# Sums of h made inside the up product and kept in DRAM, and retention's last head loading the first K tiles of its down product

## The chip, the cores and the metric

The kernel runs on 1 core of one Trainium2 chip. The metric is the device time of one execution in microseconds (us); the number compared is the median of the runs. Engines are named as in the profile: PE (TensorE, matrix products), PEld (its weight loads), DVE (VectorE), ACT (ScalarE), POOL (GpSimd), SP (SyncE, which issues nearly all the DMAs, in order).

## The reference, cut to what matters

```python
# two layers, rows = 1024 prompt frames and 32 sample frames, D = 1024, D_FF = 2816, float32
for i in range(2):
    h = rmsnorm(x, norm_mix[i])
    x = x + (retention_mixer if i == 0 else gla_mixer)(h, ...)
    x = x + conv_ffn(rmsnorm(x, norm_ffn[i]), ...)
y = rmsnorm(x, norm_final)

def retention_mixer(h, S0, pos, w_in, gn_g, w_out):      # 4 heads, dk = 256, dv = 512
    q, k, v, g = split(h @ w_in)                          # q, k rotated
    S, o = run_chunked(step, S0, (q, k, v))               # per head, chunk by chunk, with a state S
    o = (o - mean(o)) * rsqrt(var(o) + EPS) * gn_g        # per frame and head
    return (silu(g) * o) @ w_out, S                       # w_out: 2048 x 1024

def conv_ffn(h, conv_state, w_up, conv_w, conv_b, w_down):
    u = h @ w_up                                          # 1024 x 5632
    c = conv_b + sum(ext[:, j:j+T] * conv_w[j] for j in range(3))
    gate, val = split(c)
    return (silu(gate) * val) @ w_down, ext[:, T:]        # w_down: 2816 x 1024
```

The states and the last rows of each convolution are outputs too.

## The kernel before, in words

T = 1056 columns (1024 prompt, 32 sample) stand on the free axis, in four chunks `CQ` of TH = 264; features stand on the 128 partitions. Every float32 product is made of three matmuls on values split in two parts: hi times hi, hi times lo, lo times hi. A split is an ACT copy to the hi part (`CAST`) and a DVE subtraction for the lo part. So an operand is ready in two steps on two engines, and a matmul can start on the hi part when the lo part isn't there yet.

The stages in order of time, in the profiled execution:

1. Opening and the q, k, g products of retention, to 359 us.
2. Retention (`retention`), 359 to 715 us: 4 heads of 9 chunks, the last chunk of a head the 32 sample rows. `chunk` is a generator whose parts are run in turns with those of the next chunk. A head's weights `w_rv` are loaded when it starts (`Head`). After the chunks m = 1, 3, 5, 7 of each head `weight_sums_out` (L352) loads two pieces of `w_down`, makes four sums of them on DVE and stores them in the DRAM scratch `scr_w`. They use the same ring of `raw` tiles as the weight loads. The retention pool gives PSUM's eight banks in the order in which its tiles are first asked for: four to `sm`, one to `v` (psv), one to `out` (po), two to `pu`.
3. Retention's down product (`second(0)`, class `Down`, L1197), 715 to 884 us: 16 K tiles, for each chunk of 264 columns 8 output tiles, each in a PSUM bank of its own; per K tile 8 x 3 matmuls (L1260, L1261, L1262). `Down.early` (L1205) loads and splits the first two K tiles while the last chunk of retention runs. `Down.load` (L1224) loads the weights (`raw<-w_ro`) and h (`AR<-scr_or`, L1234), and splits both (L104 and L1236/L1237; `XB` is the room in which the hi and lo parts stand).
4. The up product of layer 0 (`ffn_up`, L1444), 884 to 1371 us: 22 pairs f of feature tiles, each with two halves s of the columns and 7 products for each half instead of 8 (a Strassen-Winograd scheme; `seven`, L327 to L332). A product is 12 matmuls of 264 columns. `conv` (L1470) convolves, gates, and stores h of this f in the DRAM scratch `scr_h` (L1487, L1488).
5. The down product's first 16 K tiles, in the same scheme (class `Pieces`), 1371 to 1585 us: part p = 0 takes h of f 0 to 7, part p = 1 of f 8 to 15. A unit (p, q, s) is one pair q of output tiles and one half s. Its right operands are seven blocks of h and of sums of h, split in hi and lo, in the rooms `X[s][1..7]` that lie in XA and XB. The loads of h (`staged`, L1341, 1056 KB each) and `operands` (L1343), a list of 7 splits and 4 subtractions on DVE (L1355, 128x1056 each) per s, are made at the transition: those of (p 0, s 0) in the last f of the up product, those of (p 0, s 1) in `run` before its first unit, through the same two staging rooms `SX` in the tile AR.
6. The last 6 K tiles (`Down`), 1585 to 1640 us. Then GLA and the same stages 3 to 6 for layer 1 to the end (its transition from up to down at 2637 us).

The order of the engines' instructions is set by a scheduler that knows the dependencies and the program's order; each engine then works through its list in order, and SP issues DMAs in order. The waits named below are therefore waits of a whole engine.

Of the kernel before, what the change touches and what calls it, by code (L numbers as in the profile page):

```python
# [52 lines left out]
def trunk_kernel(ctx: ExitStack, tc: tile.TileContext, io):  # L53
# [201 lines left out]
    scr_x = io["scr_x"]  # L255
    scr_w, scr_g, scr_qk = io["scr_w"], io["scr_g"], io["scr_qk"]
# [370 lines left out]
    def retention(d1):  # L627
# [13 lines left out]
        def first_loads():  # L641
# [6 lines left out]
            for c in range(2):  # L648
                c0, n = CM[c]
                for j in (1, 0):  # L650
# [3 lines left out]
                    o += 768  # L654

# [14 lines left out]
        rmask, rcol = early[:2]  # L670
        last_v = [None]
# [29 lines left out]
        def chunk(H, m):  # L701
# [68 lines left out]
            if norms:  # L770
                norms.pop()(rsm)
            po = pp.tile([P, RDV], F32, tag="out", name=f"po{i}")
# [5 lines left out]
            pu = pp.tile([P, 2, RDV], F32, tag="pu", name=f"pu{i}")  # L778
# [35 lines left out]
            if end:  # L814
                on = w_tile(f"on{i}").bitcast(F32)
                sg = w_tile(f"sg{i}").bitcast(F32)[:, :RDV]
            else:
                on = rp.tile([P, RDV], F32, tag="on", name=f"on{i}", bufs=2)
                sg = rp.tile([P, RDV], F32, tag="sg", name=f"sg{i}", bufs=3)
            sg = sg.rearrange("p (e t) -> p e t", e=4)  # L820
# [3 lines left out]
            def norm(sm):  # L824
# [3 lines left out]
                if end:  # L828
                    ot = on[:, RDV:].rearrange("p (e t) -> p e t", e=4)
                else:  # L830
                    ot = rp.tile([P, 4, P], F32, tag="ot", name=f"ot{i}", bufs=2)
# [4 lines left out]
            if m % 2 == 1:  # L836
                j = 4 * h + m // 2
# [4 lines left out]
        heads = {0: Head(0)}  # L842
        run = chunk(heads[0], 0)
        next(run)
        for n in range(len(units)):
# [8 lines left out]
            else:  # L854
                d1.early(0)
                d1.early(1)
            next(run)
            if n in (0, 2):
# [345 lines left out]
    class Down:  # L1204
        def __init__(self, nk, wsrc, hsrc, chunks, res, sm, keep, hold):  # L1205
# [4 lines left out]
        def early(self, kt):  # L1210

            c0, n = self.chunks[0]
            hr = raw_tile(f"he{uid()}")[:, :n]
            nc.sync.dma_start(hr, self.hsrc(kt)[:, c0:c0 + n])
            h = w_tile(f"hs{uid()}")
            S.copy(h[:, :n], hr)
            V.tensor_tensor(h[:, 512:512 + n], hr, h[:, :n].bitcast(F32), op=ALU.subtract)
            w = load_w(self.wsrc(kt))
            if kt in self.keep:
                self.kept[kt] = w  # L1220
            self.ops[0, kt] = w, (h, h[:, 512:])
# [18 lines left out]
        def run(self, room, evict, norm_a, norm_b, done, nxt=()):  # L1240
# [3 lines left out]
            for c, (c0, n) in enumerate(self.chunks):  # L1244
                xr = room("xr")[:, :KT * n].rearrange("p (k t) -> p k t", k=KT)
                nc.sync.dma_start(xr, self.res[:, :, c0:c0 + n])
# [585 lines left out]
```

## Time and profile before

| | |
|---|---|
| median of 3 runs | 2894.62 us (2890.69 to 2897.35) |
| the profiled execution, its own time | 2897.01 us |
| its span in the trace | 2895.2 us (1.8 us lie outside it) |
| mean granted TensorE clock | 0.988 |
| busy: PE, PEld | 2800.4 us (97%), 2695.0 us (93%) |
| busy: DVE, ACT, POOL | 2143.6 us (74%), 1333.6 us (46%), 294.0 us (10%) |
| DMA queue q1 | 399.48 MB, 41.8% of the 16 DMA engines' time |

A row of the timeline gives the start, the length, the engine, the line, the operation, `out<-in` by the program's names, the shapes, and in brackets the engine's idle time just before the instruction with what ended it. Matmuls overlap: of two that follow each other at full rate the starts lie 0.12 us apart for 264 columns, though each is recorded as 0.28 us long.

### The profile page before, as it was taken

The page shows a single profiled execution, that of the slowest core. Times are in us where ns is not written, and L with a number is a line of the kernel's source. Part 1 is how long each engine was busy: PE and PEld are TensorE (multiplying, and loading weights), DVE is VectorE, ACT ScalarE, POOL GpSimd, SP SyncE. Part 2 cuts the span into 40 slices and gives each one's busy share as a digit, 9 for nine tenths or more (in the row PEclk, how much of TensorE's full clock was granted, in tenths as well). Part 3 has the DMA queues.
Part 4 walks back from the last instruction along what each step waited for, and adds up shares of the span by engine and source line. Part 5 has one row for each costly group of instructions (what it writes and reads, how often), then busy time and mean ns, then how long its engine had stood idle before and what let it go on. Part 6 is the DMA issues. An engine that isn't in the chain of part 4 may idle for free.

```text
span 2895.2 us, 52494 instructions
## 1 busy us (share of the span) xinstructions
PE 2800.4 (97%) x20954; PEld 2695.0 (93%) x20954; DVE 2143.6 (74%) x3513; ACT 1333.6 (46%) x2401; POOL 294.0 (10%) x516
## 2 busy tenths in 40 slices
PE   8999999999999999999899999999998999998998
PEld 8999978777999999999899899999998999998997
DVE  7777777777678877777775577774498778778756
ACT  8433444443544444444443455553354444445434
POOL 1000000000000111111000132220011111111001
PEclk9999999999999999999999999999999999999999
DMA  6332377655865222223667201114642232226663
GB/s 217 105 129 96 128 233 236 196 190 164 272 214 164 76 82 89 82 75 111 227 210 240 99 22 50 51 44 150 221 154 69 74 104 71 85 74 209 216 226 117
DMA packets 224710, 403.43 MB, mean 139 GB/s; under 512 B 27056, under 2 KB 139312, under 8 KB 224464
## 3 DMA queue, kind: packets, MB, share of 16 engines
q1 hardware_dynamic: 223920, 399.48, 41.8%
q8 instruction: 164, 2.69, 0.4%
q14 instruction: 82, 0.67, 0.1%
q10 hardware_dynamic: 544, 0.59, 0.1%
HBM read 284.81 MB, written 115.20 MB: 138 GB/s over the span
## 4 chain that ended last, share of the span: by engine, by line
PE 80%; DVE 10%; DMA 5%; ACT 3%; issue 2%; POOL 1%; SPq 0%; DVEq 0%; ACTq 0%; POOLq 0%
PE pu L332 16%; PE pu L327 16%; PE pu L331 16%; PE pd L1261 3%; PE pd L1262 3%; PE pd L1260 3%; PE psv L233 1%; PE psv L231 1%; PE psv L232 1%; PE pj L124 1%; PE pj L126 1%; PE pj L125 1%; DMA AR<-scr_h 1%; DMA pv<-w_dn 1%; PE pl L983 1%
## 5 line engine op out<-in xcount | busy, mean ns | idle before, releaser
L104 DVE TENSOR_TENSOR wlo<-raw,whi 128x1024 fp32r<-128x1024 f32 x168 | 210.2, 1254 | 101.3 <-ACT whi L104 48.4
L1460 ACT COPY AR<-pu 128x264 f32<-128x264 f32 x264 | 98.8, 374 | 305.1 <-PE pu L332 302.4
L104 ACT CAST whi<-raw 128x1024 fp32r<-128x1024 f32 x168 | 175.2, 1047 | 130.9 <-PE pu L332 27.5
L332 PE MATMUL pu<-XA,wgl 128*128 128x264 f32 x752 | 213.7, 284 | 0.0
L327 PE MATMUL pu<-XA,wgh 128*128 128x264 f32 x752 | 213.1, 283 | 0.0
L331 PE MATMUL pu<-XA,wgh 128*128 128x264 f32 x752 | 213.1, 283 | 0.0
L1482 DVE SCALAR_TENSOR_TENSOR AR<-AR,cw 128x1058 f32<-128x1058 f32 x88 | 116.2, 1320 | 72.1 <-ACT AR L1481 72.0
L1261 PE MATMUL pd<-XB,whi 128*128 128x264 f32 x560 | 159.6, 287 | 2.1 <-DVE XB L1237 2.1
L1262 PE MATMUL pd<-XB,wlo 128*128 128x264 f32 x560 | 159.3, 286 | 0.0
L1260 PE MATMUL pd<-XB,whi 128*128 128x264 f32 x560 | 155.9, 286 | 0.0
L300 DVE TENSOR_TENSOR wtl<-rv,wth 128x1024 fp32r<-128x1024 f32 x58 | 71.0, 1224 | 109.6 <-ACT wth L299 107.9
L327 PE MATMUL pu<-XA,wsh 128*128 128x264 f32 x520 | 148.8, 286 | 2.5 <-DVE AR L1456 0.9
L332 PE MATMUL pu<-XA,wsl 128*128 128x264 f32 x520 | 148.6, 286 | 0.8 <-DVE wsl L300 0.8
L331 PE MATMUL pu<-XA,wsh 128*128 128x264 f32 x520 | 147.9, 284 | 0.0
L327 PE MATMUL pu<-XA,whi 128*128 128x264 f32 x448 | 129.6, 290 | 17.1 <-ACT XA L1350 15.1
L1456 DVE TENSOR_TENSOR AR<-AR,pu 128x264 f32<-128x264 f32 (+2 forms) x440 | 145.7, 371 | 0.5 <-PE pu L332 0.5
L327 PEld LDWEIGHTS pu<-XA,wgh 128*128 128x128 f32 x752 | 141.4, 188 | 0.0
L332 PEld LDWEIGHTS pu<-XA,wgl 128*128 128x128 f32 x752 | 141.3, 188 | 0.0
L331 PEld LDWEIGHTS pu<-XA,wgh 128*128 128x128 f32 x752 | 141.3, 188 | 0.0
L331 PE MATMUL pu<-XA,whi 128*128 128x264 f32 x448 | 129.0, 289 | 0.5 <-DVE XA L1351 0.5
L332 PE MATMUL pu<-XA,wlo 128*128 128x264 f32 x448 | 128.3, 289 | 0.0
L149 POOL TENSOR_TENSOR ss<-ss,sq 128x264 f32<-128x264 f32 (+2 forms) x39 | 40.9, 1049 | 758.5 <-ACT sq L138 758.5
(467 smaller groups left out, 10633.5 us busy)
## 6 DMA issues: line engine op xcount, KB each, us to landing
raw<-w_ro SPq DMA_DIRECT2D x55, 512.0 KB, 4.6
rg<-w_up SPq DMA_DIRECT2D x44, 512.0 KB, 3.5
rv<-w_up SPq DMA_DIRECT2D x44, 512.0 KB, 3.5
scr_h<-AR SPq DMA_DIRECT2D x44, 512.0 KB, 2.7
AR<-scr_h SPq DMA_DIRECT2D x16, 1056.0 KB, 5.7
AR<-scr_x SPq DMA_DIRECT2D x32, 528.0 KB, 4.9
scr_x<-AR SPq DMA_DIRECT2D x32, 528.0 KB, 3.7
raw<-scr_w SPq DMA_DIRECT2D x32, 512.0 KB, 4.4
```

What stands on the lines that cost most here:

```text
L104: ins = S.copy(hi, raw), V.tensor_tensor(lo, raw, hi.bitcast(F32), op=ALU.subtract)
L149: eng.tensor_tensor(s_[:, :n], s_[:, :n], sq[:, :n], op=ALU.add)
L300: V.tensor_tensor(l_, src, h.bitcast(F32), op=ALU.subtract)
L327: mm = PE.matmul(ps, wh[:, k], x[:, 0, kt], start=m in (1, 2, 4, 5) and kt == 0, stop=False, skip_group_check=True)
L331: PE.matmul(ps, wh[:, k], x[:, 1, kt], start=False, stop=False, skip_group_check=True)
L332: mm = PE.matmul(ps, wl[:, k], x[:, 0, kt], start=False, stop=kt == 3, skip_group_check=True)
L1260: PE.matmul(o, w[0][:, k], h[0][:, :n], start=i == 0, stop=False)
L1261: PE.matmul(o, w[0][:, k], h[1][:, :n], start=False, stop=False)
L1262: self.last_mm = PE.matmul(o, w[1][:, k], h[0][:, :n], start=False, stop=i == nk - 1)
L1456: V.tensor_tensor(u[:, d:d + n], t[:, o:o + n], b[:, o:o + n], op=op)
L1460: S.copy(t, b)
L1482: V.scalar_tensor_tensor(cj, uj[:, 1:T + 3], cw[:, nt, 1:2], cj, op0=ALU.mult, op1=ALU.add)
```

## The change

Seven things are changed.

- A new DRAM scratch `scr_s` holds the sums of h that part p = 0 of the down product needs, for each of four pairs of K tiles (k and k + 4). They are made during the up product: in f = 8, 10, 12, 14 two DMAs load h of k and k + 4 (`load_h`), in the f after it DVE makes four subtractions (`sum_h`, 128x2x264), and in the f after that one DMA stores them (`sums_out`).
- At the transition, part p = 0 no longer has the four `staged` loads and the eight L1355 subtractions. In their place stand 14 loads of 528 KB, one for each operand block (`part_one`, `pull`), four of them at a time in four slots; each split (`splits`) is a copy, a subtraction and the issue of the next load. Part p = 1 is loaded and summed as before.
- Retention's down product loads three K tiles in the last head instead of two in the last chunk: `Down.early` only issues the loads, four units before the end, and the splits come when the last chunk has run. Most of what is loaded goes to the opening's room `home`, so `raw` tiles are hardly used for it.
- With `narrow = 3`, the first chunk's K tiles 0 to 2 are first multiplied into 5 of the 8 output tiles and then into the other 3, before K tile 3 follows.
- The retention pool asks for `v`, `out` and `pu` before `sm`, so PSUM's banks are given in another order: v 0, out 1, pu 2 and 3, sm 4 to 7.
- `weight_sums_out` comes after the chunks m = 0, 2, 3, 5 of each head.
- In layer 0, x (`xT`, 1056 KB) is loaded at K tile 4 of the down product instead of ahead of it, and the convolution's columns behind it.

The first place is SP at the end of retention, from the first load for the down product's running K tiles on. Before (`o_ret_s` is the sample state's store, `ot` and `sg` are tiles of the group norm, `raw` a weight tile, `AR<-scr_or` the h of a K tile, `xT` the residual):

```order
L102 DMA raw473_7443<-w_ro 128x1024
L102 DMA raw485_7578<-w_ro 128x1024
L833 DMA scr_or<-ot463_7454 128x4x128
L821 DMA sg465_7482<-scr_g 128x4x32
L799 DMA o_ret_s<-Sn465_7468 128x2x512
L1527 DMA gn0_7497<-rgn 128x16
L1529 DMA cw0_7499<-convp 128x176
L1531 DMA cc0_7501<-cache 128x88
L102 DMA raw486_7609<-w_ro 128x1024
L1246 DMA AR0_7507<-xT 128x8x264
L1234 DMA AR0_7507<-scr_or 128x264 x2
```

The changed kernel at the same place:

```order
L803 DMA o_ret_p<-Sn464_7396 128x2x512
L833 DMA scr_or<-ot464_7411 128x4x128
L803 DMA o_ret_s<-Sn466_7456 128x2x512
L102 DMA raw489_7637<-w_ro 128x1024
L102 DMA raw490_7669<-w_ro 128x1024
L1246 DMA AR0_7512<-scr_or 128x264 x2
L1280 DMA AR0_7512<-xT 128x8x264
```

The three small loads are gone from between the sample state's store and the weights, h now goes ahead of xT, and the two weight tiles are those of K tiles 3 and 4 instead of 2 and 3 (before, `raw473` belongs to the early K tile 1).

The second place is DVE at the transition from the up product of layer 0 to the down product, as far as the first lo part that PE needs for the second half (before: the second row from the end; L1482, L1483 and L1486 are the convolution of f = 21, L1355 a sum of h, L1351 a lo part, L1456 the up product's additions):

```order
L1351 TENSOR_TENSOR XA_64<-AR0_7507,XA_64 128x1056
L1456 TENSOR_TENSOR AR0_7507<-AR0_7507,pu934_14887 128x232
L1456 TENSOR_TENSOR AR0_7507<-AR0_7507,pu934_14887 128x32
L1482 SCALAR_TENSOR_TENSOR AR0_7507<-AR0_7507,cw0_7499 128x1058
L104 TENSOR_TENSOR wlo938_15022<-raw938_15019,whi938_15021 128x1024
L1482 SCALAR_TENSOR_TENSOR AR0_7507<-AR0_7507,cw0_7499 128x1058
L1483 SCALAR_TENSOR_TENSOR AR0_7507<-AR0_7507,cw0_7499 128x1058 x2
L1355 TENSOR_TENSOR AR0_7507<-AR0_7507 128x1056
L1351 TENSOR_TENSOR XA_64<-AR0_7507,XA_64 128x1056
L1486 TENSOR_TENSOR AR0_7507<-AR0_7507 128x1058
```

The changed kernel as far as the same lo part (the last row; L1403 is now a lo part, L1549 and L1550 the convolution, L1523 the additions, L1437 and L104 lo parts of weights):

```order
L104 TENSOR_TENSOR wlo930_14801<-raw930_14798,whi930_14800 128x1024
L1437 TENSOR_TENSOR wv931_14804<-rv932_14805,wv931_14804 128x512
L1403 TENSOR_TENSOR XA_64<-AR0_7512,XA_64 128x1056
L1523 TENSOR_TENSOR AR0_7512<-AR0_7512,pu936_14923 128x232
L1523 TENSOR_TENSOR AR0_7512<-AR0_7512,pu936_14923 128x32
L1523 TENSOR_TENSOR AR0_7512<-AR0_7512,pu935_14884 128x264
L1403 TENSOR_TENSOR XB0_7516<-AR0_7512,XB0_7516 128x1056 x2
L1403 TENSOR_TENSOR XA_64<-AR0_7512,XA_64 128x1056
L1549 SCALAR_TENSOR_TENSOR AR0_7512<-AR0_7512,cw0_7506 128x1058 x2
L1550 SCALAR_TENSOR_TENSOR AR0_7512<-AR0_7512,cw0_7506 128x1058 x2
L1403 TENSOR_TENSOR XA_64<-AR0_7512,XA_64 128x1056
```

The sums are gone; two lo parts for the second half (the XB rows) have moved ahead of the convolution of f = 21, and the lo part of its first block (m = 1) stands behind the convolution in both.

The third place is PE at the same transition. Before, at the first matmuls of the second half (`pu943` is its product 1, `pu944` its product 2):

```order
L327 MATMUL pu935_14968<-XA_64,whi928_14773 128x264
L331 MATMUL pu935_14968<-XA_64,whi928_14773 128x264
L332 MATMUL pu935_14968<-XA_64,wlo928_14774 128x264
L327 MATMUL pu943_15091<-XA_64,whi926_14761 128x264
L327 MATMUL pu944_15105<-XB0_7511,whi926_14761 128x264
L331 MATMUL pu943_15091<-XA_64,whi926_14761 128x264
L332 MATMUL pu943_15091<-XA_64,wlo926_14762 128x264
```

In the changed kernel (`pu945` is product 1 of the second half and `pu946` its product 2):

```order
L332 MATMUL pu937_14997<-XA_64,whi929_14794 128x264
L333 MATMUL pu937_14997<-XA_64,wlo929_14795 128x264
L328 MATMUL pu945_15119<-XA_64,whi928_14788 128x264
L328 MATMUL pu946_15133<-XB0_7516,whi928_14788 128x264
L332 MATMUL pu946_15133<-XB0_7516,whi928_14788 128x264
L333 MATMUL pu946_15133<-XB0_7516,wlo928_14789 128x264
```

Forty other matmuls, the whole of product 2 among them, now stand between product 1's first matmul (row 9423 of PE's list) and its second, which needs the lo part (row 9464). Before, these were rows 9439 and 9441, with one between.

The diff, cut to what the prediction speaks of:

```diff
 def retention(d1):
+        for tag, shape in (("v", [P, RDV]), ("out", [P, RDV]), ("pu", [P, 2, RDV])):
+            pp.tile(shape, F32, tag=tag, name=f"first_{tag}")
...
-            if m % 2 == 1:
-                j = 4 * h + m // 2
+            if m in (0, 2, 3, 5):
+                j = 4 * h + (m + 1) // 2
                 weight_sums_out(j // 8, j // 4 % 2, j % 4)
...
-            else:
-                d1.early(0)
-                d1.early(1)
             next(run)
+            if then is None:
+                for split in first_down:
+                    split()
+            if n == len(units) - 4:
+                for kt in range(3):
...
+                    first_down.append(d1.early(kt, raw_tile("he")[:, :TH] if kt == 2 else early[-1][:, q:q + TH],
+                                               early[-1][:, o:o + D]))
 class Down:
+                    if c == 0 and i == 4:
+                        nc.sync.dma_start(xr, self.res[:, :, c0:c0 + n])
+                    if c == 0 and i < self.narrow:
+                        for nt in range(5):
+                            mm(i, nt)
+                        continue
+                    if c == 0 and i and i == self.narrow:
+                        for nt in range(5, KT):
+                            for k in range(i):
+                                mm(k, nt)
 class Pieces:
+        def load_h(self, k, after):
+            for a in range(2):
+                order(nc.sync.dma_start(self.v[:, a], scr_h[k + 4 * a].rearrange("p (q t) -> p q t", q=4)), after)
+        def sum_h(self, j):
+            b11, b12, b21, b22 = [self.v[:, a, o::2] for a in range(2) for o in range(2)]
+            d, a, b = [(b12, b12, b11), (b22, b22, b12), (b11, b22, b11), (b21, b22, b21)][j]
+            V.tensor_tensor(d, a, b, op=ALU.subtract)
+        def sums_out(self, k):
+            nc.sync.dma_start(scr_s[k].rearrange("p (a q t) -> p a q t", a=2, q=4), self.v)
+        def pull(self, n=1):
+            for _ in range(min(n, len(self.queue))):
+                s, m, src = self.queue.pop(0)
+                v = self.slots[self.at % 4]
+                self.at += 1
+                nc.sync.dma_start(v, src)
+                self.ready.append((s, m, v))
+        def splits(self):
+            def run():
+                s, m, v = self.ready.pop(0)
+                S.copy(self.X[s][m][:, 0], v)
+                V.tensor_tensor(self.X[s][m][:, 1], v, self.X[s][m][:, 0].bitcast(F32), op=ALU.subtract)
+                self.pull()
+            self.todo += [run] * 7
         def begin(self):
-            self.staged(0, 0, 1)
-            self.operands(0)
+            self.pull(2)
+            self.splits()
         def run(self):
...
-            for j in range(2):
-                self.staged(0, 1, j)
-            self.operands(1)
+            self.splits()
 def ffn_up(l, X, todo, fc, sm, nxt, after):
                 if s == 0 and i == 2:
-                    nxt.staged(0, 0, 0)
+                    nxt.part_one()
+                    nxt.pull(2)
...
+            if s == 1 and i % 2 == 0 and 8 <= f <= 16 and f % 2:
+                nxt.sum_h(i // 2)
+            if s == 0 and i == 5 and 8 <= f <= 16:
+                if f % 2 == 0:
+                    if f > 8:
+                        nxt.sums_out((f - 10) // 2)
+                    if f < 16:
+                        nxt.load_h((f - 8) // 2, stored[0])
-    d1r = Down(16, ..., range(2, 5), 4)
+    d1r = Down(16, ..., range(3, 6), 4, 3)
```

More of the change, by code (lines that the diff above doesn't have):

```diff
@@ L1336, in __init__, with part_one @@
             self.res = [AR[:, o:o + 4 * TH] for o in (8288, 8288 + 4 * TH)]
-            self.W, self.todo = {}, []
+            self.W, self.todo, self.queue, self.ready = {}, [], [], []
+            self.slots = [AR[:, SX[0] + o * 4 * TH:SX[0] + (o + 1) * 4 * TH].rearrange("p (k t) -> p k t", k=4)
+                          for o in range(4)]
+            v = AR[:, SX[0]:SX[0] + 2 * KT * 132].rearrange("p (a q t) -> p a q t", a=2, q=4)
+            self.v = v
+            self.at = 0
+        def load_h(self, k, after):
[14 more added lines that the diff above has]
+                self.ready.append((s, m, v))
+        def part_one(self):
+            for s in range(2):
+                a, b = [slice(t, t + TH) for t in (CQ[2 * s][0], CQ[2 * s + 1][0])]
+                lo, hi = scr_h[0:4], scr_h[4:8]
+                sm_ = scr_s.rearrange("k p (a t) -> k p a t", a=2)
+                for m, src in ((1, lo[:, :, a]), (2, hi[:, :, a]), (5, sm_[:, :, 0, b]), (6, sm_[:, :, 1, b]),
+                               (7, sm_[:, :, 0, a]), (4, sm_[:, :, 1, a]), (3, hi[:, :, b])):
+                    self.queue.append((s, m, src.rearrange("k p t -> p k t")))
+        def splits(self):
[5 more added lines that the diff above has]
+            self.todo += [run] * 7
         def staged(self, p, s, j):
@@ L1446, in ffn_up @@
         W, U, unit = {}, {}, {}
+        stored = [None]
         def weight_sums(f):
```

68 lines of the change are left out of this document (40 added, 28 removed).

## The prediction

> **What bounds the kernel now.** I read the page's busy shares first, then PE's list of waits, and for each wait that the change touches PE's timeline around it and the busy time by stretch. The page's first part:
>
> ```profile
> PE 2800.4 (97%) x20954; PEld 2695.0 (93%) x20954; DVE 2143.6 (74%) x3513; ACT 1333.6 (46%) x2401; POOL 294.0 (10%) x516
> ```
>
> PE is the bound nearly everywhere, and no matmul is added or taken away. So only PE's waits, and the rate at which it runs after them, can change. From the list of waits (engine, output and line, what was waited for: sum, times, longest), the rows that the change touches:
>
> ```profile
> PE pu L327 <- ACT XA L1350: 15.1, 4, 6.6
> PE pd L1260 <- ACT XB L1236: 4.3, 1, 4.3
> PE pss L719 <- DVE pm L722: 2.2, 1, 2.2
> PE pd L1260 <- ACT on L822: 2.1, 1, 2.1
> PE po L786 <- DVE vl L767: 2.0, 3, 0.8
> PE po L784 <- ACT vh L766: 1.9, 2, 1.1
> PE pd L1260 <- DVE Sn L793: 1.2, 1, 1.2
> ```
>
> Two of the four waits in the first row are the transitions from up to down product of the two layers. PE's timeline there, and at the beginning of retention's down product:
>
> ```profile
> 716.93 0.39 PE L1260 MATMUL pd<-hs,whi 128*128 128x264 f32 x1 [1.20 <-DVE Sn L793]
> 720.02 0.39 PE L1260 MATMUL pd<-hs,whi 128*128 128x264 f32 x1 [2.11 <-ACT on L822]
> 720.38 0.28 PE L1262 MATMUL pd<-hs,wlo 128*128 128x264 f32 x1
> ...
> 729.32 1.03 PE L1260 MATMUL pd<-XB 128*128 128x264 f32 x3 [4.34 <-ACT XB L1236]
> ...
> 1380.09 0.39 PE L327 MATMUL pu<-XA,whi 128*128 128x264 f32 x1 [0.96 <-ACT AR L1396]
> ...
> 1381.54 0.28 PE L332 MATMUL pu<-XA,wlo 128*128 128x264 f32 x1
> 1388.40 0.59 PE L327 MATMUL pu<-XA,whi 128*128 128x264 f32 x1 [6.59 <-ACT XA L1350]
> ...
> 2637.01 0.39 PE L327 MATMUL pu<-XA,whi 128*128 128x264 f32 x1 [0.95 <-ACT AR L1396]
> 2645.23 0.59 PE L327 MATMUL pu<-XA,whi 128*128 128x264 f32 x1 [6.49 <-ACT XA L1350]
> ```
>
> A wait costs more than its length: the clock falls behind the long ones. By stretch (busy time and count of matmuls first, then PEld, DVE, ACT, POOL, the granted clock, DMA share and GB/s):
>
> ```profile
> 729.00:736.00 7.00, 6.68 (x33) 6.68 (x34) 5.10 (x8) 4.66 (x8) 0.00 (x0) 0.55 0.85 287
> 736.00:746.00 10.00, 10.00 (x85) 10.00 (x84) 4.61 (x7) 4.08 (x6) 0.00 (x0) 1.00 0.80 262
> 1388.00:1395.00 7.00, 5.98 (x27) 5.38 (x28) 6.79 (x6) 3.66 (x5) 0.00 (x0) 0.57 0.67 235
> 1395.00:1405.00 10.00, 10.00 (x84) 10.00 (x84) 9.25 (x13) 4.89 (x6) 0.00 (x0) 1.00 0.19 57
> 2645.00:2652.00 7.00, 6.07 (x31) 5.47 (x32) 6.88 (x7) 3.48 (x5) 0.00 (x0) 0.63 0.67 234
> ```
>
> At full clock 10 us hold 84 or 85 matmuls, 0.12 us each. After the three long waits 7 us hold 33, 27 and 31 at a granted clock of 0.55 to 0.63.
>
> **Retention's end, what is lost now.** Waits 1.20 + 2.11 + 4.34 = 7.65. Then 33 matmuls take 7.00 us instead of 33 x 10/85 = 3.88; of these 3.12 us 0.32 are the wait's own end (to 729.32), so 2.8 for the clock. Together 10.45 us.
>
> The 4.34 us is K tile 2 coming late. Rows of SP, ACT and, from just before, DVE:
>
> ```profile
> 720.35 0.43 SPq L102 DMA_DIRECT2D raw<-w_ro  x1
> 720.89 0.56 SPq L1246 DMA_DIRECT2D AR<-xT  x1
> 721.50 1.19 SPq L1234 DMA_DIRECT2D AR<-scr_or  x2
> 728.86 0.72 ACT L1236 CAST XB<-AR 128x264 fp32r<-128x264 f32 x2 [3.83 <-DMA AR<-scr_or]
> 712.95 0.69 DVE L832 TENSOR_TENSOR ot<-pt,sg 128x512 f32<-128x512 f32 x1 [1.22 <-PE pt L827]
> ```
>
> The small h loads stand behind a weight tile and 1056 KB of xT, and take 7.4 us to the cast. In the changed kernel K tile 2 is loaded before and h goes ahead of xT. PE has 3 x 24 = 72 matmuls, 72 x 0.12 = 8.6 us, from about 715.5 (its first wait began at 716.93 - 1.20) to 724.1 before it asks for K tile 3. The 5 tiles done first take banks of psv and sm, so that neither Sn's bank (1.20) nor the group norm's (2.11) is asked for until 715.5 + 45 x 0.12 = 720.9. By then both are read: the waits for them ended at 716.93 and 720.02 before, give or take the splits now put ahead of them.
>
> The cover is not free. Three lo parts (two of 128x1024, 1.2 us each by the L300 row further down, and one of 128x264, some 0.4) now stand ahead of the last chunk's vh. DVE idled 1.22 us there before, so some 1.6 us are left, of which PE, with work of the chunk before it, may see 0.5, an estimate. The lo part of K tile 2 comes behind Sn: another 0.5. K tile 3's h is issued at about 719, by 1024 KB of weights behind it in the queue at 287 GB/s (3.7 us) it lands at 723 to 724 and is split by 724.8: 0.5. K tile 5's weights stand behind xT: 0 to 3, I take 1.5. So 3.0 of the 10.45 come back: **-7.5**, with ends of -3.3 (only the first two waits go) and -10.4.
>
> **The two transitions, what is lost now.** Layer 0: 0.96 + 6.59, then 27 matmuls in 7.00 us instead of 27 x 10/84 = 3.21, less the 0.40 us of wait in that stretch: 3.39. Together 10.94. Layer 1: 0.95 + 6.49 + (7.00 - 3.69 - 0.23 = 3.08) = 10.52. What DVE does meanwhile:
>
> ```profile
> 1368.22 1.26 DVE L1355 TENSOR_TENSOR AR<-AR 128x1056 f32<-128x1056 f32 x1 [1.69 <-DMA AR<-scr_h]
> ...
> 1384.02 1.32 DVE L1482 SCALAR_TENSOR_TENSOR AR<-AR,cw 128x1058 f32<-128x1058 f32 x1
> 1385.25 2.55 DVE L1483 SCALAR_TENSOR_TENSOR AR<-AR,cw 128x1058 f32<-128x1058 f32 x2
> 1387.71 1.26 DVE L1355 TENSOR_TENSOR AR<-AR 128x1056 f32<-128x1056 f32 x1
> 1388.88 1.26 DVE L1351 TENSOR_TENSOR XA<-AR,XA 128x1056 fp32r<-128x1056 f32 x1
> ```
>
> From 1368.22 to 1390.1 DVE works without a pause. Taking the sums away is therefore a real relief, and so is loading the second half earlier; but in DVE's order product 1's lo part still stands behind the convolution of f = 21. I add up the changed order from product 5's lo part of the first half, which waits for its load until about 1367.5 (before, DVE was held by such a load until 1368.22). Eight lo parts at 1.17 from start to start make 9.4, four convolution steps at 1.23 4.9, and, estimated from their sizes, two weight lo parts 2.3, the gate times value product of the convolution before 1.2, a half weight tile 0.6 and the up product's last additions 1.9: 20.3 us, so 1387.8. PE stood at the second half's product 1 at 1381.66 and now has 25 more matmuls to do before it needs that lo part (row 9464 instead of 9439): 1381.66 + 25 x 0.12 = 1384.7. It waits 3.1 us instead of 6.59. How the clock answers to 3.1 us is open. It kept its rate after 1.20 and 2.11 (the row of 720.38 is 0.28 long), but not after two waits in part p = 1:
>
> ```profile
> 1478.70 0.39 PE L327 MATMUL pu<-XA,whi 128*128 128x264 f32 x1 [1.86 <-ACT XA L1350]
> 1479.67 0.59 PE L327 MATMUL pu<-XB,whi 128*128 128x264 f32 x1 [0.58 <-ACT XB L1350]
> ...
> 1480.38 0.42 PE L332 MATMUL pu<-XA,wlo 128*128 128x264 f32 x1
> ...
> 1482.58 0.39 PE L331 MATMUL pu<-XB,whi 128*128 128x264 f32 x1
> ```
>
> From 1480.38 to 1482.58 ten matmuls take 0.22 us each, 1.0 us too much; after 4.34 us of wait it was 2.8. I take 2.0 for 3.1. With the 0.96 left and 0.5 for product 5's late block, 6.5 of 10.94 stay: -4.4, and in layer 1 -4.0. Together **-8.4**, with ends of 0 and -21.5.
>
> On the clock the Trainium skill has a rule of its own ("TensorE: Matmul & The Clock Gate", Part 1: The HAM clock gate): TensorE drops to half rate after an idle window of about 3.4 us, and comes back after as long a busy one. By that rule waits of 3.1 us would leave the clock alone and the sum would be 4 us lower; the slow matmuls after 1.86 and 0.58 us above speak against it, so the rows decide.
>
> **The additions in the up product.** Per layer 16 subtractions of 128x2x264 (near the 128x512 form's 0.69 us, quoted below) are 11 us of DVE, and DVE has room:
>
> ```profile
> 884.00:1371.00 487.00, 483.81 (x3966) 482.09 (x3965) 386.30 (x566) 228.66 (x323) 60.53 (x147) 1.00 0.28 91
> 1086.26 1.23 DVE L300 TENSOR_TENSOR wtl<-rv,wth 128x1024 fp32r<-128x1024 f32 x1 [2.70 <-ACT wth L299]
> 1090.48 1.32 DVE L1482 SCALAR_TENSOR_TENSOR AR<-AR,cw 128x1058 f32<-128x1058 f32 x1 [1.89 <-ACT AR L1481]
> ```
>
> Idle DVE time is 101 us here, and in each f's 20 us it has gaps of 2.70 and 1.89 us. The DMAs (8 loads of 528 KB, 4 stores of 1056 KB) go at a share of 0.28, a whole f ahead of their use, and SP passes them in order behind the stores of h. Cost 0; if the first sum of each of the four groups met an unlanded load, up to 2 us each.
>
> **Retention's other edits.** The 2.23 us at its start (`pm` behind other work on DVE) are due to order; the weight sums there now come ahead of the next refill, at the price of about 0.6 for the new first banks: **-1.6**, ends 0 and -2.2. Moving the weight sums removes those of m = 7 from ahead of the next head's weights (the vl and vh rows above, 3.9 us in all) and puts two in neighbouring chunks:
>
> ```profile
> 409.18 0.69 DVE L358 TENSOR_TENSOR pv<-pv 128x512 f32<-128x512 f32 x1 [3.66 <-DMA pv<-w_dn]
> ```
>
> In that place DVE stood 3.66 us for such a load. I take 0, ends -3.9 and +4.
>
> **The sum.** 2897.0 (the profiled execution) - 7.5 - 8.4 - 1.6 = 2879.5. The profiled execution lies 2.4 above the median of the runs, which would be 2877.1 by the same sum; I forecast **2878**, its own range 2871 to 2887.
>
> **The rivals.**
> 1. *The transition vanishes nearly whole*: product 1's lo part comes before PE needs it, for instance because the scr_s load doesn't hold DVE. Then 3.1 + 2.0 more go in each layer: 2878 - 10.2 = 2868. For it: PE has three products that are ready. Against it: DVE's added-up 20.3 us. Chance 0.12.
> 2. *The 3.1 us stay but the clock holds*: 2878 - 4 = 2874. For it: 2.11 us did no harm. Against it: the rows of 1480. Chance 0.10. (It is what the Trainium skill's rule of Part 1 would give.)
> 3. *The wait only moves*: in the first half each block now waits for its own load, two at a time at first, and DVE, held by them, is as late as before at the convolution. Only retention's 9.1 us are won: 2894.6 - 9.1 = 2885.5. For it: DVE had been held 1.69 us for a load already. Chance 0.17.
> 4. *It does nothing measurable*: besides, retention's wait moves whole from K tile 2 to K tile 3, only 1.2 + 2.1 are won: 2894.6 - 3.3 = 2891.3. Chance 0.08.
> 5. *Slower*: weight sums in neighbouring chunks. The second's loads wait in SP for the first's stores, since they share the `raw` ring, and DVE stands before its first sum. Eight of these (m = 2 and 3 in four heads) at 3.66 us are 29 us if PE has nothing to go on with: 2878 + 29 = 2907. It decides from 17.5/8 = 2.2 us each. For it: the row of 409.18. Against it: PE lost only 0.8 us there. Chance 0.08.
>
> **How the numbers follow.** The forecast has 0.45. A measurement here tells a change from none at about 0.2%, 5.8 us: faster is below 2888.8, slower above 2900.4. Faster are the forecast, rivals 1 and 2 and three quarters of rival 3, 0.80, less 0.02 for the forecast's tail: 0.78. Same are rival 4 and the rest, 0.14. Slower is rival 5, 0.08. The range 2864 to 2893 holds all but rival 5, about half of rival 4 and the ends of the retention terms.
>
> **What would show it right or wrong.** PE's timeline after retention should show no wait over 1.5 us until K tile 5, and a granted clock near 1.0 there; one of 4 us at K tile 3 would break that term. At 1384 to 1388 PE should wait about 3 us for a lo part (DVE XA L1403), not for a hi part. The list of waits should have no new row of DVE for the scr_h loads in the up product, and the row of DVE pv L358 should stay near its sum. A time above 2893 would mean retention's weight sums or the up product pay for it.

## The result, and the profile after

| | before | after |
|---|---|---|
| median | 2895.34 us (2890.69 to 2897.35, 4 runs) | 2874.53 us (2871.20 to 2878.57, 4 runs) |
| ratio, 95% interval | | 0.9931 (0.9913 to 0.9949) |
| the profiled execution, its span | 2897.01, 2895.2 us | 2871.20, 2869.3 us |

The change makes the kernel 20 us faster (0.69%, 0.51 to 0.87%). The forecast was 2878, range 2864 to 2893. The two profiled executions lie 25.9 us apart, more than the medians, since the one of after is the lowest of its runs. The page's first row after, then the rows of PE's list of waits that answer to those of before:

```profile
PE 2791.4 (97%) x20954; PEld 2687.3 (94%) x20954; DVE 2145.1 (75%) x3529; ACT 1332.3 (46%) x2401; POOL 277.8 (10%) x516
...
PE pu L328 <- ACT XA L1418: 3.0, 2, 1.6
PE pt L831 <- DVE AR L1662: 2.9, 1, 2.9
PE pt L831 <- ACT on L826: 2.4, 3, 1.6
PE pd L1273 <- ACT XB L1248: 1.4, 1, 1.4
PE po L790 <- DVE vl L771: 0.6, 2, 0.3
```

The waits for XA have gone from 15.1 to 3.0 us: the two at the transitions (6.59 and 6.49) are no longer there, what is left are waits in part p = 1. Those for vl went from 2.0 to 0.6, and the rows for pm, Sn and ACT's vh are gone. But two rows are there that before did not have, both for pt, the transposes of retention's group norm: 2.9 us for DVE at the last one, and 2.4 us in three places for ACT. I followed the two places of the change through PE's timeline and the stretches. Before, the last chunk's po and the up product's first wait:

```profile
714.48 0.42 PE L780 MATMUL po<-vh,ph 128*32 128x512 f32 x1 [0.18 <-DVE vh L251]
...
928.58 0.39 PE L327 MATMUL pu<-XA,wsh 128*128 128x264 f32 x1 [0.94 <-DVE AR L1456]
```

After, from the same po to the same wait:

```profile
708.74 0.42 PE L784 MATMUL po<-vh,ph 128*32 128x512 f32 x1 [0.34 <-DVE vh L251]
...
719.66 0.39 PE L1273 MATMUL pd<-XB 128*128 128x264 f32 x1 [1.40 <-ACT XB L1248]
720.96 0.59 PE L1274 MATMUL pd<-XB 128*128 128x264 f32 x1 [0.90 <-DVE XB L1249]
...
763.47 0.43 PE L831 MATMUL pt<-ident,on 32*128 32x32 f32 x4 [2.89 <-DVE AR L1662]
...
921.68 0.39 PE L328 MATMUL pu<-XA,wsh 128*128 128x264 f32 x1 [0.99 <-DVE AR L1523]
```

The stretches behind those waits (columns as before):

```profile
719.00:726.00 7.00, 5.43 (x24) 5.23 (x25) 2.83 (x5) 2.69 (x6) 0.00 (x0) 0.60 1.03 379
726.00:736.00 10.00, 10.00 (x80) 10.00 (x80) 6.23 (x9) 5.85 (x10) 0.00 (x0) 0.94 0.77 261
764.00:774.00 10.00, 10.00 (x71) 10.00 (x72) 6.97 (x14) 3.72 (x9) 4.19 (x5) 0.83 0.98 308
```

The last chunk's po begins at 708.74 instead of 714.48: retention itself is 5.7 us ahead. The up product's first wait, the same in both kernels, ends at 921.68 instead of 928.58, 6.9 us ahead. So of what the end of retention and its down product were to bring, 1.2 us is left in these two traces: K tile 3 costs 1.40 + 0.90 us and then a clock of 0.60 (the 7 us from 719 hold 24 matmuls), and the end of the first chunk 2.89 us and a clock of 0.83.

At the transition of layer 0, the SP row of the first block of sums, then rows of DVE up to the lo part that PE needed 3 us earlier by my sum, and PE:

```profile
1344.59 0.37 SPq L1387 DMA_DIRECT2D AR<-scr_s  x1
1355.70 1.25 DVE L1403 TENSOR_TENSOR XA<-AR,XA 128x1056 fp32r<-128x1056 f32 x1
...
1371.76 2.70 DVE L1549 SCALAR_TENSOR_TENSOR AR<-AR,cw 128x1058 f32<-128x1058 f32 x2
1374.37 2.55 DVE L1550 SCALAR_TENSOR_TENSOR AR<-AR,cw 128x1058 f32<-128x1058 f32 x2
1376.83 1.25 DVE L1403 TENSOR_TENSOR XA<-AR,XA 128x1056 fp32r<-128x1056 f32 x1
1380.33 0.39 PE L328 MATMUL pu<-XB,whi 128*128 128x264 f32 x1 [0.58 <-ACT AR L1462]
1382.78 0.39 PE L333 MATMUL pu<-XA,wlo 128*128 128x264 f32 x1 [0.73 <-DVE wlo L104]
```

And the stretch behind it:

```profile
1385.00:1395.00 10.00, 10.00 (x84) 9.93 (x83) 7.42 (x12) 3.76 (x6) 0.00 (x0) 1.00 0.94 324
```

No wait there reaches 1 us, and the clock is 1.00. Layer 1's transition looks the same: its longest wait is 0.79 us, at 2627.63.

### The profile page after: what moved, and what is told of

It is laid out like the page before. It is cut to its first block, busy times and chain, and to the rows that moved or that the text cites. A ratio compares the mean times of both kernels' runs of the same rounds, so it can differ in the third digit from the quotient of the medians.

```text
span 2869.3 us, 52602 instructions
## 1 busy us (share of the span) xinstructions
PE 2791.4 (97%) x20954; PEld 2687.3 (94%) x20954; DVE 2145.1 (75%) x3529; ACT 1332.3 (46%) x2401; POOL 277.8 (10%) x516
## 4 chain that ended last, share of the span: by engine, by line
PE 80%; DVE 9%; DMA 4%; ACT 3%; issue 2%; POOL 1%; SPq 0%; DVEq 0%; ACTq 0%; POOLq 0%
PE pu L333 16%; PE pu L328 16%; PE pu L332 16%; PE pd L1274 3%; PE pd L1275 3%; PE pd L1273 3%; PE psv L233 2%; PE psv L232 2%; PE psv L231 2%; PE pj L124 1%; PE pj L126 1%; PE pj L125 1%; PE pg L124 1%; PE pg L125 1%; PE pg L126 1%
## 5 line engine op out<-in xcount | busy, mean ns | idle before, releaser
L104 DVE TENSOR_TENSOR wlo<-raw,whi 128x1024 fp32r<-128x1024 f32 x161 | 201.3, 1253 | 97.3 <-ACT whi L104 46.0
L104 ACT CAST whi<-raw 128x1024 fp32r<-128x1024 f32 x161 | 167.8, 1047 | 118.4 <-DMA raw<-w_ro 26.7
L1549 DVE SCALAR_TENSOR_TENSOR AR<-AR,cw 128x1058 f32<-128x1058 f32 x88 | 115.9, 1318 | 58.5 <-ACT AR L1548 55.9
L1523 DVE TENSOR_TENSOR AR<-AR,pu 128x264 f32<-128x264 f32 (+2 forms) x440 | 144.6, 368 | 0.0
L328 PE MATMUL pu<-XA,wth 128*128 128x264 f32 x408 | 116.3, 285 | 0.1
```

Of the source, the lines that this page charges most:

```text
L104: ins = S.copy(hi, raw), V.tensor_tensor(lo, raw, hi.bitcast(F32), op=ALU.subtract)
L328: mm = PE.matmul(ps, wh[:, k], x[:, 0, kt], start=m in (1, 2, 4, 5) and kt == 0, stop=False, skip_group_check=True)
L1523: V.tensor_tensor(u[:, d:d + n], t[:, o:o + n], b[:, o:o + n], op=op)
L1549: V.scalar_tensor_tensor(cj, uj[:, 1:T + 3], cw[:, nt, 1:2], cj, op0=ALU.mult, op1=ALU.add)
```

## The experiments

After the traces the theory was: the transitions are nearly all of the gain (17 us), the moved weight sums give about 5, and the rest of retention's edits give back what they gain. The rival was the sum on record: transitions 8.4, end of retention 7.5, its beginning 1.6, weight sums 0. Each run was timed against the kernel before on the same chip; the ratio is turned into us at 2893.

| run | what it is | ratio, 95% interval | us against before |
|---|---|---|---|
| a_sums | sums of h and 14 loads only | 0.9943 (0.9931 to 0.9955) | -16.5 |
| b_ret | all of retention's edits only | 1.0007 (0.9997 to 1.0017) | +2.0 |
| c_wsums | weight sums' place only | 0.9980 (0.9972 to 0.9988) | -5.8 |
| d_unused | sums of h made, not used | 1.0001 (0.9991 to 1.0010) | +0.3 |
| e_sums_ws | a_sums and c_wsums | 0.9927 (0.9915 to 0.9940) | -21.1 |
| f_early | b_ret without c_wsums | 1.0018 (1.0008 to 1.0028) | +5.2 |
| g_xt | the change, later xT held back | 0.9924 (0.9912 to 0.9936) | -22.0 |
| h_first | the change, h ahead of weights | 0.9946 (0.9933 to 0.9959) | -15.6 |
| i_xt | e_sums_ws, every xT at K tile 4 | 0.9907 (0.9895 to 0.9919) | -26.9 |
| j_bank | i_xt with the new bank order | 0.9911 (0.9898 to 0.9923) | -25.7 |
| k_max | a_sums with DVE's steps put back | 0.9993 (0.9984 to 1.0002) | -2.0 |
| f_xt | f_early, later xT held back | 1.0007 (0.9997 to 1.0017) | +2.0 |

**a_sums.** The edit: before, with the change's `scr_s`, `load_h`, `sum_h`, `sums_out`, `part_one`, `pull`, `splits` and their calls.

```diff
-            self.staged(0, 0, 1)
-            self.operands(0)
+            self.pull(2)
+            self.splits()
```

> Only the sums of h in DRAM and the transition's 14 loads; retention and its down product as before. Theory from the two traces (the transitions are nearly all of the gain): both waits of 6.5 us and the slow clock behind them go, 9 us in layer 0 and 8 to 9 in layer 1, so 17 us faster than before, about 2878. Theory as predicted (DVE still late by 3.1 us per layer): 8.4 us faster, about 2886. In the trace the first says: PE's longest wait within 15 us of either transition is below 1.5 us and the second half's first split is not waited for; the second says 3 us there.

Measured 2877.23 us (2872.07 to 2880.39): the first theory. The sums of h and their loads are 16 of the change's 20 us. PE's waits near the transition of layer 0:

```profile
1384.30 0.39 PE L328 MATMUL pu<-XB,whi 128*128 128x264 f32 x1 [0.52 <-ACT AR L1438]
1386.82 0.39 PE L333 MATMUL pu<-XA,wlo 128*128 128x264 f32 x1 [0.79 <-DVE wlo L104]
```

**b_ret.** The edit: before, with all the other hunks of the change (retention, `Down`, the convolution's columns). In `Down` the later load of x is not bound to layer 0: the first chunk of every down product, GLA's and the last 6 K tiles' too, loads it at K tile 4.

> Only retention's edits: early K tiles, narrow, bank order, weight sums after m = 0, 2, 3, 5, xT later; sums of h as before. Theory from the traces (the end of retention gives its gain back in a slow clock at K tile 3 and a wait at the first chunk's end, the heads gain about 5): 6 us faster, about 2889. Theory as predicted: 7.5 at the end and 1.6 at the beginning, 9 us faster, about 2886. Both transitions' waits of 6.5 us stay in either.

Measured 2893.38 us (2887.61 to 2902.17, 12 runs): neither theory; nothing is gained. Its profiled execution was the lowest of its 12 runs, 5.8 us below their median, and by its trace alone I would have believed in a gain.

**c_wsums.** The edit:

```diff
-            if m % 2 == 1:
-                j = 4 * h + m // 2
+            if m in (0, 2, 3, 5):
+                j = 4 * h + (m + 1) // 2
```

> Before, with the weight sums after m = 0, 2, 3, 5 of each head and nothing else. Theory from the traces (the waits for vh and vl at the changes of head and for pm at the first chunk were the weight sums' doing): 4 to 5 us faster, about 2891. Theory as predicted (0, ends -3.9 and +4): no difference, 2895. If the bank order is needed too, no difference either, and the waits for vh and vl stay in the trace.

Measured 2886.74 us, 5.8 us faster (3.5 to 8.1): the first theory, a little more than it said, and without the bank order. In PE's list the row for pm and that for vh at the changes of head are gone, and a new one is there for the group norm; what stands there of it and of vl:

```profile
PE pt L827 <- ACT on L822: 2.3, 2, 1.7
...
PE po L786 <- DVE vl L767: 0.4, 1, 0.4
```

DVE's wait for the loads of these sums falls too, from 14.3 us in 8 waits to this:

```profile
DVE pv L358 <- DMA pv<-w_dn: 4.7, 5, 2.0
```

PE's waits in retention are so about 3 us shorter in sum; what the other 3 of the 5.8 us are was not traced.

**d_unused.** The edit: before, with `load_h`, `sum_h` and `sums_out` and their calls in the up product, and nothing that reads `scr_s`.

> Before, with the sums of h made and stored in the up product and not used: the transition loads and sums as before, so this is the price of the added 32 subtractions, 16 loads and 8 stores alone. Both theories: 0, within 2 us of before, since DVE idles 101 us per layer there and the DMAs are a share of 0.28. A rival (they hold up the weights of the next f): up to 2 us for each of the eight groups, 5 to 16 us slower.

Measured 2893.31 us, 0.3 us above before (-2.6 to +2.9). The additions cost nothing that can be measured; the rival of 5 to 16 us is out.

**e_sums_ws.** The edit is that of a_sums and that of c_wsums.

> The sums of h in DRAM and the weight sums after m = 0, 2, 3, 5, and nothing else of the change. If the two gains measured alone (16 and 6 us) are of different places they add up: 22 us faster than before, about 2871, and a little faster than the whole change, whose other edits then give nothing. If the other edits do gain when the weight sums are moved, this is slower than the whole change: 2877 or more.

Measured 2871.13 us: 16.5 and 5.8 add up to 22.3, measured 21.1. Three of the seven changes (the sums of h, the 14 loads and the place of the weight sums) account for all of the gain.

**f_early.** The edit: b_ret with the weight sums after m = 1, 3, 5, 7.

> Retention's edits without the moved weight sums: early K tiles, narrow, bank order, xT later. By the difference of two runs (all of retention's edits 0.5 us slower, the weight sums alone 6 us faster) this is 6 us slower than before, about 2899. As predicted (the end of retention gains 7.5): 7 us faster, about 2886. If the two parts don't add up: between.

Measured 2898.19 us, 5.2 us slower than before (2.3 to 8.1). So these edits, taken together, cost time. Part of it is at the end of retention: from the last chunk's po to the up product's first wait it takes 214.7 us, where the other executions with the old code there, but for before's own, take 210.6 to 212.4. PE's waits in its down product:

```profile
724.25 0.39 PE L1272 MATMUL pd<-XB 128*128 128x264 f32 x1 [1.74 <-ACT XB L1247]
725.54 0.59 PE L1273 MATMUL pd<-XB 128*128 128x264 f32 x1 [0.90 <-DVE XB L1248]
731.41 0.39 PE L1273 MATMUL pd<-XB 128*128 128x264 f32 x1 [0.91 <-DVE XB L1248]
736.79 1.23 PE L1272 MATMUL pd<-XB 128*128 128x264 f32 x8 [2.31 <-ACT XB L1247]
770.55 0.43 PE L830 MATMUL pt<-ident,on 32*128 32x32 f32 x4 [2.42 <-DVE AR L1610]
```

K tiles 3, 4 and 5 come late one after the other, and pt waits at the end of the first chunk as in the whole change. The reading that PE, with three tiles ready, comes sooner to those that aren't fits these rows; no run tests it alone.

**g_xt.** The edit, in the whole change:

```diff
-                if c:
-                    nc.sync.dma_start(xr, self.res[:, :, c0:c0 + n])
...
-                    if c == 0 and i == 4:
-                        nc.sync.dma_start(xr, self.res[:, :, c0:c0 + n])
+                    if i == 4:
+                        x_in = nc.sync.dma_start(xr, self.res[:, :, c0:c0 + n])
+                        if c:
+                            order(x_in, self.last_mm)
```

> The whole change, with xT of the second to fourth chunk issued at that chunk's own K tile 4 rather than as early as its room is free. Theory: the 2.9 us at the end of the first chunk (a bank waited for behind a late weight tile) come of two loads of xT, 2112 KB, ahead of the weights within the first chunk; then that wait goes and the slow clock behind it, 4 us faster than the whole change, about 2870. Rival: the weights are late because the first chunk needs more than the DMA can bring anyway; then the wait stays and the time is that of the whole change, 2874.

Measured 2871.60 us; the interval overlaps that of the whole change, so the time alone doesn't decide. The trace does for the mechanism. In the whole change SP issued xT three times within the first chunk:

```profile
714.04 0.66 SPq L1280 DMA_DIRECT2D AR<-xT  x1
...
736.87 0.56 SPq L1259 DMA_DIRECT2D AR<-xT  x1
...
748.41 0.56 SPq L1259 DMA_DIRECT2D AR<-xT  x1
```

With the later two held back, pt at the first chunk's end waits only 0.18 us, and the clock stays up:

```profile
754.00:764.00 10.00, 10.00 (x84) 9.93 (x82) 6.48 (x9) 5.47 (x9) 0.00 (x0) 1.00 0.84 258
764.00:774.00 10.00, 9.82 (x82) 9.65 (x81) 7.80 (x16) 4.27 (x10) 4.17 (x5) 1.00 0.85 265
```

From the last chunk's po to the wait in the up product it takes 206.4 us, where the whole change took 921.68 - 708.74 = 212.9.

**h_first.** The edit: in `Down.load` the load and split of h are written ahead of those of the weights.

```diff
+            hr = self.room("hr")[:, :n]
+            nc.sync.dma_start(hr, self.hsrc(kt)[:, c0:c0 + n])
...
             if kt not in self.keep:
                 w = load_w(self.wsrc(kt))
...
-            hr = self.room("hr")[:, :n]
-            nc.sync.dma_start(hr, self.hsrc(kt)[:, c0:c0 + n])
```

> The whole change, with h loaded and split ahead of the weights of each K tile in the down products. Theory: K tile 3 waits 1.40 + 0.90 us because its h is cast on ACT behind the weights of K tile 5; then these waits shrink to below 1 us in sum, the clock keeps its rate in the 7 us behind them, and 3 to 5 us go: about 2870. Rival: h itself lands late, the wait stays, 2874.

Measured 2878.17 us, not faster. It doesn't test the theory: the scheduler put the first h casts behind the third weight cast all the same. ACT's rows there:

```profile
717.73 1.04 ACT L104 CAST XB<-raw 128x1024 fp32r<-128x1024 f32 x1 [0.28 <-DMA raw<-w_ro]
718.68 0.72 ACT L1242 CAST XB<-AR 128x264 fp32r<-128x264 f32 x2
722.45 0.78 ACT L1242 CAST XB<-AR 128x264 fp32r<-128x264 f32 x2 [3.05 <-DMA AR<-scr_or]
```

The whole change has the same order:

```profile
718.25 1.04 ACT L104 CAST XB<-raw 128x1024 fp32r<-128x1024 f32 x1 [0.61 <-DMA raw<-w_ro]
719.21 0.72 ACT L1248 CAST XB<-AR 128x264 fp32r<-128x264 f32 x2
```

**i_xt.** The edit: that of e_sums_ws, with K tiles loaded as before and xT as in g_xt for all four chunks.

> Sums of h in DRAM, weight sums after m = 0, 2, 3, 5, two early K tiles as before, and xT of every chunk of the down products issued at that chunk's K tile 4. Theory (2112 KB of xT ahead of the first chunk's weights cost about 3 us, in the old layout too): 3 us faster than the sums and weight sums alone, 2868. Rival (in the old layout the first chunk's xT only made K tile 2 late, and the later ones came at a time that did no harm): no difference from 2871.

Measured 2867.48 us (2865.04 to 2871.68), 26.9 us faster than before (23.4 to 30.4), and the lowest median. That is 5.8 us more than e_sums_ws by the ratios, whose intervals just overlap, so the theory has the sign and the trace for it rather than a time clear of noise. From the last chunk's po to the up product's first wait it takes 207.4 us, where e_sums_ws took 212.4. The edit holds for every down product, and the last 6 K tiles of layer 0 are shorter too, 79.0 us (1532.24 to 1611.28) instead of 81.7. PE's waits from the last chunk on are those for Sn and the group norm, unchanged, and K tile 2 is no longer waited for:

```profile
713.13 0.39 PE L1260 MATMUL pd<-hs,whi 128*128 128x264 f32 x1 [1.21 <-DVE Sn L794]
716.23 0.39 PE L1260 MATMUL pd<-hs,whi 128*128 128x264 f32 x1 [2.12 <-ACT on L823]
...
918.07 0.39 PE L328 MATMUL pu<-XA,wsh 128*128 128x264 f32 x1 [0.93 <-DVE AR L1502]
```

**j_bank.** The edit: i_xt with `first_v`, `first_out`, `first_pu` and pu asked for ahead of po, as in the change.

> The kernel of i_xt with the change's bank order as well. Theory: the waits of 1.2 us for Sn and 2.1 us for the group norm at the first output tiles go, so 3 us faster than i_xt. Rival: PE then waits as much for K tile 2, whose loads are what sets the time there; no difference from i_xt.

Measured 2868.67 us: no difference from i_xt, the rival. In its trace the 1.2 us for Sn is gone and 2.11 for the group norm stays, followed by 0.91 at K tile 2.

**k_max.** The edit, in a_sums:

```diff
+                if m in (5, 6, 7, 4):
+                    V.tensor_tensor(v, v, v, op=ALU.max)
                 S.copy(self.X[s][m][:, 0], v)
```

> Only the sums of h in DRAM, with one added DVE operation of 128x1056 in place (a maximum of a block with itself, so the values stay) ahead of each split of products 4 to 7: it puts the eight DVE steps per layer that the change removed back in their place and leaves the earlier loads. Theory that DVE's relief is the cause: most of the 16 us come back, 2886 or more. Theory that the earlier loads of the second half are: 2877 to 2880, as without the added steps.

Measured 2891.84 us, by the ratios 14.5 us above a_sums: DVE's relief is the cause. The loads of the first half are issued within 1 us of those in a_sums. Those of the second half begin at 1372.30, 5 us behind a_sums (1367.06), since a slot comes free only when DVE has split what is in it, but 6 us ahead of before (1378.72). So earlier loads without the relief bring nothing that can be measured (-2.0, from -4.6 to +0.6). PE's waits and stretches at the transition of layer 0:

```profile
1380.69 0.59 PE L328 MATMUL pu<-XA,whi 128*128 128x264 f32 x1 [3.32 <-ACT XA L1380]
...
1389.27 0.39 PE L328 MATMUL pu<-XB,whi 128*128 128x264 f32 x1 [2.47 <-ACT XB L1380]
```

```profile
1375.00:1385.00 10.00, 6.65 (x40) 6.44 (x41) 9.60 (x11) 5.83 (x7) 1.64 (x4) 0.83 1.03 335
1385.00:1395.00 10.00, 7.29 (x43) 6.67 (x42) 9.95 (x10) 4.78 (x6) 0.00 (x0) 0.83 0.73 239
```

These 20 us hold 83 matmuls, where the same 20 us of a_sums hold 140 (69 and 71), so PE falls some 7 us behind (57 x 0.12), by waits and by the clock, and DVE is busy for 19.55 of the 20 us. The eight steps of 1.17 us in each layer cost 14.5 us in the two layers.

**f_xt.** The edit is that of g_xt, in f_early.

> Retention's edits without the moved weight sums (measured: 5 us slower than before), with xT of the second to fourth chunk held back to that chunk's K tile 4. Theory: the hoisted xT is the larger part of that loss, so 3 to 5 us of it go, 2893 to 2895, and no wait of PE for a bank at the end of the first chunk. Rival (the early K tiles or narrow themselves cost it): 2898.

Measured 2895.08 us, at the upper end of the theory's 2893 to 2895, but the intervals of f_early and f_xt overlap, and the theory's sign isn't there: pt still waits 1.72 us for DVE at the end of the first chunk, at 771.08. So that the hoisted xT is a part of what f_early loses is possible and not shown. It isn't the whole: PE still waits for K tiles 3 and 4 (1.64 us at 725.79 and 1.51 us at 731.61).

## Why the prediction was right, and where it wasn't

The sign and the size were right, by terms that were not: the transitions and the weight sums together gained 14 us more than the sum had for them (8.1 and 5.8), and the rest of retention's edits gained 14 us less (+5.2 where it had -9.1). That these errors nearly cancel, and the forecast lies 3.5 us from the median, is luck.

- *The transitions*, put at -8.4: a_sums gave -16.5 (13.0 to 20.0). The mechanism was right (k_max: DVE's eight steps decide it) and the size wrong. The step that failed is "product 5's lo part of the first half, which waits for its load until about 1367.5". I had put that load at the time when before's second load of the first half let DVE go on (issued at 1362.56); but a slot was free, and SP issued it at 1344.59. The lo part began at 1355.70, which is 1362.6 on before's clock (6.9 us), 4.9 us earlier than I had it. From there to the end of product 1's lo part it took 22.4 us, where I had added up 20.3; the steps were those I had counted, and DVE was idle for 1.7 us between them. That end, at 1378.1, is where PE needs it (its matmul starts at 1378.14, 0.1 us late), and the 3.1 us of wait and the 2.0 us of clock that I left in each layer vanish. Rival 1 had it so, for the reason given there, with a chance of 0.12.
- *The end of retention*, put at -7.5: f_early, which holds this and the -1.6, was 5.2 us slower. Two steps failed. "by 1024 KB of weights behind it in the queue [...] it is split by 724.8" counted the DMA and little else. On after's clock (5.7 us earlier) that would be 719.1; but h's cast only began at 719.21, right behind ACT's third weight cast, which had waited for the weights of a K tile further on, and its lo part, behind a weight's on DVE, let PE go on only at 720.96. The 2.3 us of wait are not much more than the 0.5 and 1.5 that I put on K tiles 3 and 5, but the clock behind them costs another 2.6 in this execution (26 matmuls follow 0.22 us apart instead of 0.12), and of that the sum had nothing. Of the signs that I had named, no wait over 1.5 us before K tile 5 came true, and a clock near 1.0 did not. The weights ahead of that h in SP's order are those of K tiles 4 and 5, and not of 3 and 4 as I read the order (K tile 3's were issued at 672.15); so K tile 5's don't stand behind xT, and PE didn't wait for it. The other step, "Waits 1.20 + 2.11 + 4.34 = 7.65. Then 33 matmuls take 7.00 us", took one execution for the rule. The profiles of a_sums, c_wsums, d_unused, e_sums_ws and k_max, in which this stage is as before, show 1.95, 1.62, 1.15, 2.65 and 2.21 us in the place of the 4.34, and 210.6 to 212.4 us from the last chunk's po to the wait in the up product, where the profile of before has 928.58 - 714.48 = 214.1. So about 3 of the 10.45 us that I counted as lost were not lost as a rule.
- What I did not see at all: pt. Its transposes need a bank, all eight are held by the first chunk, and the eviction that frees one (L1662) stands on DVE behind the lo parts of two weights (L104) whose loads came late:

```profile
759.89 1.23 DVE L104 TENSOR_TENSOR wlo<-raw,whi 128x1024 fp32r<-128x1024 f32 x1 [5.36 <-ACT whi L104]
...
761.86 1.22 DVE L104 TENSOR_TENSOR wlo<-raw,whi 128x1024 fp32r<-128x1024 f32 x1
762.99 1.10 DVE L1662 TENSOR_TENSOR AR<-AR,pd 128x264 f32<-128x264 f32 x3
```

It cost 2.89 us and a clock of 0.83.
- *Retention's weight sums*, put at 0 with ends -3.9 and +4, and *its beginning*, put at -1.6: c_wsums alone gave -5.8. The waits for ACT's vh and for pm were the weight sums' doing, at the changes of head and at the beginning: they are gone from every profile with the sums moved, and f_early and f_xt, with the sums in the old place, still have them. For vl that isn't so clear (3.5 us in g_xt). That neighbouring chunks would cost (rival 5) was wrong: DVE's waits for pv fell.
- *The additions in the up product*, put at 0: d_unused gave +0.3. The row that I had named as a sign against it is in after's list all the same, for the added subtractions (L1377), in waits so short that they cost nothing:

```profile
DVE AR L1377 <- DMA AR<-scr_h: 4.7, 10, 0.7
```

- *The clock*: I priced it from single executions, and equal waits do not slow it equally. After 1.40 and 0.90 us at K tile 3, 26 matmuls of after followed 0.22 us apart; after 1.10 and 0.90 us in g_xt it was 16, and after 0.99 and 0.90 us in b_ret none. That before "kept its rate after 1.20 and 2.11" was the exception: after nearly the same two waits (1.20 to 1.22 and 2.10 to 2.29 us) 13 to 22 matmuls went 0.22 us apart in a_sums, c_wsums, d_unused, e_sums_ws, k_max and i_xt. The stretches are b_ret's behind K tile 3, and those behind the 2.1 us in before and in i_xt:

```profile
719.00:726.00 7.00, 5.20 (x40) 5.00 (x41) 3.07 (x6) 2.89 (x6) 0.00 (x0) 1.00 1.06 389
...
720.00:725.00 5.00, 4.96 (x39) 4.75 (x39) 1.23 (x1) 2.06 (x2) 0.70 (x3) 1.00 0.81 234
...
716.00:721.00 5.00, 4.77 (x26) 4.77 (x27) 1.23 (x1) 2.06 (x3) 0.84 (x3) 0.66 0.77 212
```

By the rule of the Trainium skill ("TensorE: Matmul & The Clock Gate", Part 1: The HAM clock gate), half rate after an idle window of about 3.4 us, none of these waits alone would be long enough; as in the rows of 1480, the measurement decides. What makes the difference between equal waits is open.

What stays open: which of the early K tiles, `narrow` and the bank order makes f_early slower. The bank order is not it by itself (j_bank, beside two early K tiles), and xT may be a part (f_xt, g_xt); the other two were not tried apart. Nor was it tried to let ACT cast h first. Stages that the edits don't touch differ between single traces too. From the last matmul of layer 0's down product to the first of GLA's it took 425.9 us in k_max (1631.24 to 2057.13) and 430.5 in f_early (1634.97 to 2065.46), and such spreads are in every difference of two single traces.

## What to carry to other kernels

Where an engine that is idle for a fifth of one stage is the bound of the few us between two stages, work that doesn't depend on the border is worth moving across it: the eight DVE steps of a layer cost 7 to 8 us at the transition, and the sixteen smaller ones that replace them in the up product cost nothing. Preparing more tiles ahead of a stage that the DMA feeds here moved the wait to the first tile that wasn't prepared; look also at what is queued ahead of the tile that is late (here 1056 KB of residual, needed only when a chunk ends). And a stall read from one profile is a sample: read it in every trace at hand in which that stage is the same before you put it into a sum.

## What the runs showed of the hardware

A wait need not be long to slow TensorE, and equal waits do not slow it equally. After 1.40 and 0.90 us, 26 matmuls followed 0.22 us apart instead of 0.12 (after, granted clock 0.60 over 7 us); after 0.99 and 0.90 us at the same place none did (b_ret, 1.00). After a wait of 2.1 us before kept its rate, while in six other executions 13 to 22 matmuls went at 0.22 us. Executions of one kernel differ by up to 15 us (2887.61 to 2902.17 in 12 runs of b_ret), so that a profiled execution can lie 6 us from its kernel's median.
